# First input projection of a two-layer diffusion backbone: which queue stores the results, and where the second half of the tokens gets its split weights

## The chip, the cores and the metric

One core of a Trainium2 chip runs the whole program. The metric is device time in microseconds (us). The engines are PE (TensorE, matrix products), ACT (ScalarE), DVE (VectorE), POOL (GpSimd) and SP (SyncE, which here only starts DMA transfers). Each engine takes its instructions in order; a DMA transfer is started by the queue of the engine whose name stands in front of `dma_start` (`nc.sync` is SP, `nc.scalar` is ACT).

## The reference

Two layers over 2048 latent tokens and 256 context tokens of 1024 channels. The change lies in the first layer's input projection:

```python
h  = rms_norm(x,  norm_g) * (1 + scale)  + shift
hc = rms_norm(xc, norm_g) * (1 + cscale) + cshift
u  = h @ w_in            # 1024 x 2816; hc the same
a_val, a_gate, q, k, v, z = split(u)      # 512, 512, 512, 128, 128, 1024 columns
q = axial_rope(rms_norm(q, qn_g)); k = axial_rope(rms_norm(k, kn_g))
y_b = attention(q, [ck, k], [cv, v])
y_a = silu(layer_norm(dwconv(a_val * sigmoid(a_gate), 31 taps)))
x = x + gate * (([y_a, y_b] * silu(z)) @ w_out)
```

The second layer (Fourier mixing beside neighbourhood attention) is not touched.

## The kernel before

**Products in three passes.** Every float32 operand of the projection is split into a high part (a rounded copy) and a low part (what is left), both in PE's faster float32 format; a product is high x high + high x low + low x high. For a weight, `load_w` (L383) does this for 256 columns, in two halves of the rows (`kh`): SP loads 512 KB into `wraw` (L390), ACT makes the copy `whi` (L430) and POOL the difference `wlo` (L431). Pool `wp` has four buffers each of `whi` and `wlo`, that is the weights of two tasks; pool `rp` has two of `wraw`, one task.

**Tasks.** `ab_proj` (L434) goes over the 18 tiles of 128 tokens in two halves of three blocks of 384 tokens. In each half eleven tasks (L656) run over the half's blocks, each with 256 columns of the weight: g and u (gate and value of the convolution, twice each), kv (keys and values), q (twice, four heads each) and z (the output gate, four times). The first half's g 0 and u 0 are not in the task loop: they run while the modulation is still being computed, with `w_gu` as their weights. At its start a task takes the weights `ws` that the task before it asked for, and asks for the next task's (`ws_next`). Since every task runs in both halves, each weight is loaded and split twice.

**What a task does with its sums.** g, u and z are six groups of 24 products into one of five PSUM banks (`mm_tile`, L462). ACT evicts a z group with SiLU into `tz` (two buffers), and SP stores it in `gz_d` (L694). In kv and q a group is one tile of 128 tokens; `qk` (L715) takes it through a chain on ACT, DVE and POOL (norm, rotary table `tab` loaded by SP in L719, split), transposes it on PE, and copies it to `sg` on ACT (L759). SP stores v (L752), the queries (L763, four stores a tile) and the keys (L765).

**Convolution.** When both u groups are there, 31 taps per channel group run on DVE (`conv`, L508; L517 is one tap over 1151 or 1168 tokens). They are fed into the stream between the groups of the tasks, some three per group (`advance`, L500; the rates are in L569).

**End of the stage.** At z 0 of the second half `load_kv` (L768) loads keys and values for attention from DRAM into space that the q/k chain has left, again from SP. Attention's first work on DVE is the running maximum L864.

**Order.** The program is written in one order and a planner that simulates the engines fixes each engine's stream ahead of time; within a stream nothing overtakes, on the SP queue neither. Instructions that are ready early may stand well ahead of their place in the text.

Of the kernel before, what the change touches and what calls it, by code (L numbers as in the profile page):

```python
# [20 lines left out]
P = 128  # L21
# [28 lines left out]
def dft_tables():  # L50
    """Cosines and sines of 512 rows for the even and the odd frequencies, and those of a channel group."""
    n, k = np.arange(512, dtype=np.int64), np.arange(1024, dtype=np.int64)
    a = (np.outer(n, k) % 2048) * (2 * np.pi / 2048)
    m = np.arange(128, dtype=np.int64)
    b = (np.outer(m, m) % 128) * (2 * np.pi / 128)
    seq = np.stack([f(a[:, odd::2]) for odd in range(2) for f in (np.cos, np.sin)])
    chan = np.stack([np.cos(b), np.sin(b)])
    return np.ascontiguousarray(seq.astype(np.float32)), chan.astype(np.float32)


class Stream:
    """What is due on each engine in the coming steps."""

# [20 lines left out]
class Build:  # L84
# [56 lines left out]
    def setup(self):  # L141
# [29 lines left out]
        self.gate_d = [self.dram(f"gate{a}", [2, D]) for a in range(2)]  # L171
        self.pat_d = self.dram("pat_d", [9, HEADS, P, 512])

    def x_tile(self, i):
# [3 lines left out]

# [1 line left out]
    def conditions(self, sp, pp, tag):  # L180
# [36 lines left out]
    def adaln(self, layer, j, raw, psum, mo, brow=None):  # L217
        """256 columns of the shift, scale and gate of one layer: in four steps.

        Four column tiles hold sums over a quarter of the rows each, for both conditions.  # L220
        """
        nc, I = self.nc, self.I
# [39 lines left out]

# [1 line left out]
    W0 = [0, 8, 24, 32]  # L264
# [45 lines left out]

# [1 line left out]
    def prep(self, pools, layer, sources, conds, name, eng=None):  # L312
# [70 lines left out]
    def load_w(self, raw_of, wp, w, n0, scale=1.0, eng=None, hold=None, load=True):  # L383
        """High and low parts of 256 columns of a weight, as two halves of its rows."""
        nc = self.nc
        out = []
        for kh in range(2):
            raw = raw_of(kh)
            if load:
                nc.sync.dma_start(  # L390
                    raw, w[kh * 512 : kh * 512 + 512, n0 : n0 + 256].rearrange("(k p) n -> p k n", p=P)
                )
            if scale != 1.0:
                nc.gpsimd.tensor_scalar(out=raw, in0=raw, scalar1=scale, scalar2=1.0, op0=ALU.mult, op1=ALU.mult)
            hi = wp.tile([P, 4, 256], F32R, name="whi", tag="whi")
            lo = wp.tile([P, 4, 256], F32R, name="wlo", tag="wlo")
            if hold is None:
                self.split(hi[:], lo[:], raw, eng or nc.gpsimd)
            else:
                hold.append((hi[:], lo[:], raw, eng or nc.gpsimd))  # L400
            out.append((hi, lo))
        return out

    def raws(self, pool):
        return lambda kh: pool.tile([P, 4, 256], F32, name="wraw", tag="wraw")[:]

    def mm_channel(self, ps, w, h, c, cols, ks=range(KT)):
        """ps[128 channels, tokens] from weight columns c*128.. and a block's columns."""
        nc = self.nc
# [22 lines left out]

# [1 line left out]
    def ab_proj(self):  # L434
# [5 lines left out]
        with ExitStack() as es:  # L440
# [134 lines left out]
            def ada_tiles():  # L575
                """Where the modulation's weights wait, 256 columns at a time: in tiles that nothing else needs yet."""
                quarter = lambda t: t.rearrange("p (k n) -> p k n", n=256)
# [60 lines left out]
            for b in range(3):  # L638
# [8 lines left out]
                for c in range(2):  # L647
                    glu(0, c, b, us[c], sums[1, c, b])
                nxt[b] = hl[b]
            small()  # L650
            ea.close()
# [6 lines left out]
            for half in range(2):  # L658
                blocks = range(3 * half, 3 * half + 3)
                for ti, (kind, j) in enumerate(tasks):  # L660
                    if half == 0 and ti < 2:
                        continue
                    ws = ws_next
                    if half * 11 + ti < 21:
                        nk, nj = tasks[(ti + 1) % 11]
                        ws_next = self.load_w(self.raws(rp), wp, w, col[nk] + 256 * nj)
                    if kind in "guz":
                        for f in late:
# [14 lines left out]
                        for c, b in order:  # L683
# [7 lines left out]
                            else:  # L691
                                t = zp.tile([P, 384], F32, name="tz", tag="tz")
                                nc.scalar.activation(t[:], ps[:, :384], AF.Silu)
                                nc.sync.dma_start(self.gz_d[2 * j + c, :, b * 384 : b * 384 + 384], t[:])  # L694
                            if last and c == 1:
# [19 lines left out]
    def qk(self, qp, q2, q3, sp, pt_p, rope_d, ps, tt, kind, j, nh):  # L715
# [33 lines left out]
        if kind == "kv":  # L749
            vv = q2.tile([P, P], F32, name="vv", tag="vv")  # L750
            nc.scalar.activation(vv[:], ps[:, 128:256], AF.Copy)
            nc.sync.dma_start(self.v_d[tt], vv[:])  # L752
        yield 1
# [7 lines left out]
        if kind == "q":  # L761
            for h in range(4):
                nc.sync.dma_start(self.qs_d[4 * j + h][:, ts], sg[:, h])  # L763
        else:
            nc.sync.dma_start(self.k_d[:, :, ts].rearrange("a p t -> p a t"), sg[:, :2])  # L765

# [1 line left out]
    def load_kv(self):  # L768
        """Keys as [high; high] and as [low; four rows of ones], and values."""
        nc = self.nc  # L770
# [18 lines left out]
    def ab_attention(self):  # L789
        """Scores with the keys on partitions, shifted by each query's greatest score.  # L790

        A unit is two heads of one group for 256 queries. Its greatest scores come from products of one pass, with
        the queries on partitions, a unit ahead; they are rounded and go into the scores as four more rows of the
        contraction, one for each 128 queries.
        """
        nc = self.nc
        with ExitStack() as es:
# [56 lines left out]
            def chunk(i, qt, c):  # L854
                """Part of the least (negated) score of 128 queries."""
                b, hp = units[i]
# [53 lines left out]
            def add(i, k):  # L910
                """Sums over the keys: one on DVE, one on Pool."""
                s = state[i]
# [31 lines left out]
            def total(i):  # L944
                """A row of sums, which DMAs put on 128 partitions for the reciprocals, and copy to all for the products."""
                s = state[i]
# [120 lines left out]

# [1 line left out]
    def load_wout_part(self, raw, w, k, n, eng):  # L1069
        """One block of the rows of half of an output projection's columns."""  # L1070
        ins = self.nc.sync.dma_start(raw, w[k * P : (k + 1) * P, n * 512 : n * 512 + 512])
# [20 lines left out]
    def out_norm(self, psum, b):  # L1092
        """Layer norm and SiLU of the convolution of 256 tokens."""
        nc = self.nc
# [57 lines left out]
    def out_gate(self, b):  # L1152
        """Gates 256 tokens of both branches and splits them."""
        nc = self.nc
# [90 lines left out]

# [1 line left out]
    def cd_proj(self):  # L1247
# [86 lines left out]

# [1 line left out]
    # Rows n and 2048-n, then n and 1024-n, are folded together, so that 512 rows are left for the even and for  # L1336
    # the odd frequencies of the cosine and of the sine part; row 512 is added as a vector of signs.
    def fourier_early(self, psum):
        """What is ready before the last input projections are: channel tables, a table, the first two groups."""
        nc, I = self.nc, self.I  # L1340
# [23 lines left out]
    def fold(self, g, gp, psum):  # L1364
        """A group's folded rows after the channel transform, with rows on partitions."""
        nc = self.nc
# [47 lines left out]
    def dft_table(self, q, rp):  # L1414
        """A quarter of the table of the sequence transform, split."""
        nc = self.nc
# [61 lines left out]

# [1 line left out]
    def natten(self):  # L1480
        nc = self.nc
        with ExitStack() as es:
# [73 lines left out]
            def scores(u):  # L1556
                """The steps of a unit's scores; each gives back its eviction."""
                h, t = u
# [127 lines left out]
            def first_block():  # L1686
                """Gates and splits what is ready of the first block of the output projection."""
                bias.close()
# [45 lines left out]
    def stream(self, q, units, scores, counts, steps, transposes, multiply, lag, off, gap, extra=None):  # L1734
        """Runs the scores of later units beside the products of earlier ones, in a fixed order on each engine."""
        nc = self.nc
# [33 lines left out]

# [1 line left out]
    def cd_out(self):  # L1772
# [101 lines left out]
```

## Time and profile before

| | us |
|---|---|
| runs, fastest, median, slowest of three | 2945.24, 2954.23, 2960.78 |
| profiled execution, span from first to last instruction | 2944.6 |
| of it: start, up to the end of the first products | 0 to 92 |
| of it: tasks of the first projection | 92 to about 740 |
| of it: attention of the first layer and all that follows | from about 740 |

The tables of the profile list an instruction by its line, engine and operation, then output and inputs by the program's names, and a count. In square brackets stands the time that the engine stood idle before it, and what ended that. A line of a helper (L430 and L431, for instance) can serve many places; the names of the tiles tell them apart.

### The profile page before, as it was taken

To read this page: it belongs to the slowest core of one execution; us is meant where nothing else is said; L and a number is where in the kernel's file an instruction comes from. 1 tells how busy PE (TensorE), PEld (TensorE's weight loads), DVE (VectorE), ACT (ScalarE), POOL (GpSimd) and SP (SyncE) were. 2 spreads that over 40 slices of the span, in tenths; PEclk is the share of its full clock that TensorE was granted. 3 is DMA by queue.
4 is the path that set the end of the run, shared out by engine and by line. 5 is a ranking of instruction groups with operands and counts; after the bars stand their busy time and mean duration, and the time that the engine had idled before them with its cause. 6 is when DMAs were issued, how large, how long until landed. Compare 5 with 4: busy or idle time off the path is not lost.

```text
span 2944.6 us, 40977 instructions
## 1 busy us (share of the span) xinstructions
PE 2764.9 (94%) x14481; PEld 2128.3 (72%) x14481; DVE 1855.9 (63%) x2867; ACT 1134.3 (39%) x2103; POOL 1531.5 (52%) x1173
## 2 busy tenths in 40 slices
PE   7988799986999999999999999999999997998998
PEld 5988799886444444444445887988898886888787
DVE  4798869896877788888887564101211336777663
ACT  3223131320354555555554223123222335777421
POOL 3568624846465788778785754222122312455343
PEclk9999899998999999999999999999999998999999
DMA  8224131361642343331123653433333349999852
GB/s 249 91 77 147 53 106 47 96 179 36 196 136 78 123 138 101 90 121 55 51 63 106 235 166 136 150 127 106 126 140 128 111 152 238 220 246 225 273 197 89
DMA packets 345752, 397.66 MB, mean 135 GB/s; under 512 B 54844, under 2 KB 270444, under 8 KB 340555
## 3 DMA queue, kind: packets, MB, share of 16 engines
q1 hardware_dynamic: 344971, 390.85, 44.9%
q10 hardware_dynamic: 576, 4.19, 0.4%
q8 instruction: 114, 1.87, 0.3%
q14 instruction: 91, 0.75, 0.1%
HBM read 270.34 MB, written 129.78 MB: 136 GB/s over the span
## 4 chain that ended last, share of the span: by engine, by line
PE 65%; DMA 11%; DVE 9%; POOL 6%; issue 4%; ACT 1%; SPq 0%; POOLq 0%; ACTq 0%; DVEq 0%
PE av L900 9%; PE s L885 9%; PE mm L415 7%; PE mm L417 7%; PE mm L416 7%; PE m L862 6%; DVE acc L517 5%; DMA nv<-v_d 4%; POOL wlo L431 4%; PE mo L1087 3%; PE mo L1086 3%; PE mo L1085 3%; DMA nk<-k 3%; PE mm L424 2%; PE mm L426 1%
## 5 line engine op out<-in xcount | busy, mean ns | idle before, releaser
L431 POOL TENSOR_TENSOR wlo<-wraw,whi 128x1024 fp32r<-128x1024 f32 x86 | 323.8, 3774 | 499.7 <-ACT whi L430 481.1
L864 DVE TENSOR_REDUCE ast<-m 128x1 f32<-128x512 f32 (+1 forms) x656 | 398.7, 626 | 176.8 <-PE m L862 174.5
L890 ACT ACTIVATE pr<-s 128x512 f32<-128x512 f32 x584 | 343.1, 595 | 298.6 <-PE s L885 253.9
L925 POOL TENSOR_TENSOR accp<-accp,pr 128x512 f32<-128x512 f32 x283 | 398.7, 1409 | 88.1 <-ACT pr L890 74.2
L517 DVE SCALAR_TENSOR_TENSOR acc<-u,cw,acc 128x1151 f32<-128x1151 f32 (+1 forms) x240 | 366.5, 1582 | 0.0
L900 PE MATMUL av<-pr,vt 128*64 128x512 f32 x1168 | 317.4, 622 | 0.0
L417 PE MATMUL mm<-hi_ab,wlo 128*128 128x384 f32 x768 | 260.6, 341 | 39.1 <-POOL wlo L431 39.1
L415 PE MATMUL mm<-hi_ab,whi 128*128 128x384 f32 x768 | 261.0, 346 | 11.6 <-DVE qraw L729 7.2
L416 PE MATMUL mm<-lo_ab,whi 128*128 128x384 f32 x768 | 261.7, 342 | 0.0
L415 PE MATMUL mm<-hi_cd,whi 128*128 128x512 f32 x640 | 250.8, 392 | 1.1 <-ACT hi_cd L379 1.1
L416 PE MATMUL mm<-lo_cd,whi 128*128 128x512 f32 x640 | 250.1, 391 | 0.4 <-DVE lo_cd L380 0.4
L417 PE MATMUL mm<-hi_cd,wlo 128*128 128x512 f32 x640 | 246.7, 390 | 0.0
L417 PEld LDWEIGHTS mm<-hi_ab,wlo 128*128 128x128 f32 x768 | 147.5, 192 | 39.8 <-POOL wlo L431 39.8
L925 DVE TENSOR_TENSOR accd<-accd,pr 128x512 f32<-128x512 f32 x165 | 165.7, 1004 | 0.9 <-ACT pr L890 0.5
L1642 DVE TENSOR_TENSOR nlo<-npt,nhi 128x512 fp32r<-128x512 f32 x192 | 123.6, 644 | 62.1 <-ACT nhi L1640 61.4
L862 PEld LDWEIGHTS m<-k1h,q 128*128 128x128 f32 x328 | 62.2, 190 | 132.9 <-DVE ast L864 84.9
L415 PEld LDWEIGHTS mm<-hi_ab,whi 128*128 128x128 f32 x768 | 147.5, 193 | 14.1 <-DVE qraw L729 7.6
L1604 POOL TENSOR_SCALAR npr<-npr,nst 128x640 f32<-128x640 f32 (+1 forms) x128 | 108.1, 858 | 89.8 <-DVE nst L1603 66.7
L371 DVE TENSOR_SCALAR ht<-ptr,scale,shift 128x384 f32<-128x384 f32 (+2 forms) x96 | 61.2, 671 | 147.4 <-PE ptr L368 146.7
L862 PEld LDWEIGHTS m<-k0h,q 128*128 128x128 f32 x328 | 63.3, 195 | 125.0 <-DVE ast L864 80.6
L430 ACT ACTIVATE whi<-wraw 128x1024 fp32r<-128x1024 f32 x88 | 92.9, 1059 | 148.3 <-PE mm L416 135.5
L416 PEld LDWEIGHTS mm<-lo_ab,whi 128*128 128x128 f32 x768 | 147.8, 193 | 0.8 <-DVE lo_ab L380 0.8
(321 smaller groups left out, 7002.1 us busy)
## 6 DMA issues: line engine op xcount, KB each, us to landing
wraw<-in_cd_w_in_dram SPq DMA_DIRECT2D x46, 512.0 KB, 4.0
wraw<-in_ab_w_in_dram SPq DMA_DIRECT2D x42, 512.0 KB, 3.5
pat_d<-big SPq DMA_DIRECT2D x72, 256.0 KB, 3.7
nk<-k SPq DMA_DIRECT2D x32, 576.0 KB, 12.7
pat<-pat_d SPq DMA_DIRECT2D x24, 768.0 KB, 6.5
nv<-v_d SPq DMA_DIRECT2D x128, 128.0 KB, 7.0
adaraw<-in_ab_w_ada_dram SPq DMA_DIRECT2D x24, 512.0 KB, 6.1
adaraw<-in_cd_w_ada_dram SPq DMA_DIRECT2D x24, 512.0 KB, 3.7
```

Source lines behind the costliest of these rows:

```text
L415: nc.tensor.matmul(ps, a, hh[:, k, cols], start=k == 0, stop=False)
L416: nc.tensor.matmul(ps, a, hl[:, k, cols], start=False, stop=False)
L417: nc.tensor.matmul(ps, b, hh[:, k, cols], start=False, stop=k == KT - 1)
L431: (eng or nc.vector).tensor_tensor(out=lo, in0=src, in1=hi.bitcast(F32), op=ALU.subtract)
L517: ins = nc.vector.scalar_tensor_tensor(out=acc[:, :n], in0=u[:, tap : tap + n], scalar=cw[:, ch, tap : tap + 1], in1=acc[:, :n], op0=ALU.m ...
L862: nc.tensor.matmul(ps[:, :n], lhs, kt[hp // 2][0][:, a : a + n], start=True, stop=True)
L864: nc.vector.tensor_reduce(out=s["st"][:, qt, col : col + 1], in_=ps[:, :n], axis=AX.X, op=ALU.min)
L885: nc.tensor.matmul(ps[:], kt[hp // 2][key][:, k * P : k * P + P], s[x][:].rearrange("p j n -> p (j n)"), start=key == 0, stop=key == 1,)
L890: nc.scalar.activation(pr[:], ps[:], AF.Exp, scale=-1.0)
L900: nc.tensor.matmul(s["av"][x * 64 : x * 64 + 64], vt[:, k - 1 + x, kv * 64 : kv * 64 + 64], s["pr"][k - 1 + x][:], start=k == 1, stop=k == ...
L925: eng.tensor_tensor(out=s[name][:], in0=first_in[:], in1=s["pr"][k][:], op=ALU.add)
L1642: return lambda: nc.vector.tensor_tensor(out=lo[:, :o], in0=pt[:, :o], in1=hi[:, :o].bitcast(F32), op=ALU.subtract)
```

## The change

- The results of the projection, in `gz_d`, `v_d`, `qs_d` and `k_d`, are stored from ACT's queue instead of SP's.
- In the first half each task also stores its split weights in DRAM, four stores of 512 KB (`keep_w`, from SP): high and low part of each half of the rows.
- In the second half, and for the task that leads into it, the next task's weights are read back from there in four loads (`kept_w`, from SP); nothing is loaded raw and nothing is split.

Comment lines and docstrings that went with it are left out here.

```diff
+        self.w_d = [self.dram(f"w_d{i}", [2, 2, P, 1024]) for i in range(11)]
...
+    def keep_w(self, dst, ws):
+
+        for kh, parts in enumerate(ws):
+            for x, t in enumerate(parts):
+                self.nc.sync.dma_start(dst[x, kh], t[:].bitcast(F32).rearrange("p k n -> p (k n)"))
+
+    def kept_w(self, wp, src):
+        out = []
+        for kh in range(2):
+            parts = [wp.tile([P, 4, 256], F32R, name=n, tag=n) for n in ("whi", "wlo")]
+            for x, t in enumerate(parts):
+                self.nc.sync.dma_start(t[:].bitcast(F32).rearrange("p k n -> p (k n)"), src[x, kh])
+            out.append(tuple(parts))
+        return out
...
+            for i in range(2):
+                self.keep_w(self.w_d[i], w_gu[i])
             small()
...
                     ws = ws_next
-                    if half * 11 + ti < 21:
-                        nk, nj = tasks[(ti + 1) % 11]
+                    if half == 0:
+                        self.keep_w(self.w_d[ti], ws)
+                    nk, nj = tasks[(ti + 1) % 11]
+                    if half * 11 + ti < 10:
                         ws_next = self.load_w(self.raws(rp), wp, w, col[nk] + 256 * nj)
+                    elif half * 11 + ti < 21:
+                        ws_next = self.kept_w(wp, self.w_d[(ti + 1) % 11])
...
-                                nc.sync.dma_start(self.gz_d[2 * j + c, :, b * 384 : b * 384 + 384], t[:])
+                                nc.scalar.dma_start(self.gz_d[2 * j + c, :, b * 384 : b * 384 + 384], t[:])
...
-            nc.sync.dma_start(self.v_d[tt], vv[:])
+            nc.scalar.dma_start(self.v_d[tt], vv[:])
...
-                nc.sync.dma_start(self.qs_d[4 * j + h][:, ts], sg[:, h])
+                nc.scalar.dma_start(self.qs_d[4 * j + h][:, ts], sg[:, h])
...
-            nc.sync.dma_start(self.k_d[:, :, ts].rearrange("a p t -> p a t"), sg[:, :2])
+            nc.scalar.dma_start(self.k_d[:, :, ts].rearrange("a p t -> p a t"), sg[:, :2])
```

## The prediction

> **What bounds the kernel now.** I read the page first, then the busy time of each engine by stage, then the list of waits inside the stage that the change touches, and last the timeline around the two longest waits of TensorE.
>
> ```profile
> span 2944.6 us, 40977 instructions
> PE 2764.9 (94%) x14481; PEld 2128.3 (72%) x14481; DVE 1855.9 (63%) x2867; ACT 1134.3 (39%) x2103; POOL 1531.5 (52%) x1173
> ```
>
> PE is busy 94% of the span, but a mean over stages hides where the rest is. The same by stage (first projection's start, its main part, everything behind it); columns after the stretch and its length are busy PE, PEld, DVE, ACT, POOL with instruction counts, then granted clock, DMA share and GB/s:
>
> ```profile
> 0.00:92.00 92.00, 71.14 (x465) 59.10 (x466) 43.59 (x102) 31.99 (x60) 34.55 (x68) 0.98 0.74 222
> 92.00:740.00 648.00, 568.57 (x3635) 560.33 (x3633) 531.99 (x618) 157.52 (x331) 378.51 (x224) 0.94 0.31 93
> 740.00:2944.00 2204.00, 2125.19 (x10384) 1508.84 (x10384) 1280.34 (x2148) 944.80 (x1712) 1118.43 (x881) 0.98 0.49 144
> ```
>
> The projection runs to about 740 us. From 92 to 740 PE is idle for 648 - 568.6 = 79.4 us: all that an edit of this stage can win by filling gaps. Behind it PE is idle 79 us in 2204, so what the projection saves should reach the end. What holds PE up is in the list of waits of that stretch (us in total, times, longest) and, in order of time, at its two longest gaps:
>
> ```profile
> PE mm L417 <- POOL wlo L431: 39.1, 2, 23.7
> ACT tz L693 <- DMA gz_d<-tz: 71.4, 7, 38.7
> ```
>
> ```profile
> 355.58 0.69 PE L417 MATMUL mm<-hi_ab,wlo 128*128 128x384 f32 x1 [15.38 <-POOL wlo L431]
> 708.30 0.69 PE L417 MATMUL mm<-hi_ab,wlo 128*128 128x384 f32 x1 [23.74 <-POOL wlo L431]
> ```
>
> Two waits make 39.1 of the 79.4 us, one in each half of the tokens, both at the start of the last gate task (z 3). The instruction that ends them, first as a group (shortest, median and longest in ns), then the two themselves, and VectorE beside the second:
>
> ```profile
> L431 POOL TENSOR_TENSOR wlo<-wraw,whi x86: 2349/2402/47767, 97.6 to 2358.5; 128x1024 fp32r<-128x1024 f32 x86
> 313.82 41.71 POOL L431 TENSOR_TENSOR wlo<-wraw,whi 128x1024 fp32r<-128x1024 f32 x1 [18.83 <-ACT whi L430]
> 660.48 47.77 POOL L431 TENSOR_TENSOR wlo<-wraw,whi 128x1024 fp32r<-128x1024 f32 x1 [24.31 <-ACT whi L430]
> 627.64 78.41 DVE L517 SCALAR_TENSOR_TENSOR acc<-u,cw,acc 128x1168 f32<-128x1168 f32 x55
> 735.22 0.76 DVE L864 TENSOR_REDUCE ast<-m 128x1 f32<-128x256 f32 x2 [29.17 <-PE m L862]
> ```
>
> The low part of z 3's weights is a subtraction on GpSimd, 2.40 us by its median; these two took 41.71 and 47.77 us. Both lie in an unbroken run of convolution taps on VectorE: 55 taps in 78.41 us from 627.64, and GpSimd's instruction ends at 708.25, 2.2 us after the last tap. GpSimd gets nowhere while VectorE has no gap.
>
> **What the change removes.** The second half splits no weights: its 22 subtractions on GpSimd and 22 copies on ScalarE go. First term: the 23.74 us wait at 708.30. The 15.38 us of the first half stay, since that half still splits.
>
> ```profile
> 425.00:498.00 73.00, 73.00 (x429) 73.00 (x428) 54.77 (x42) 11.13 (x15) 23.48 (x6) 1.00 0.14 44
> 498.00:602.00 104.00, 90.26 (x707) 88.41 (x706) 93.38 (x147) 31.64 (x83) 79.83 (x76) 0.93 0.33 96
> 660.00:706.00 46.00, 24.57 (x142) 24.25 (x140) 46.00 (x35) 4.68 (x9) 45.52 (x1) 0.81 0.10 35
> 706.00:738.00 32.00, 27.50 (x146) 27.10 (x146) 2.75 (x7) 2.94 (x6) 4.57 (x2) 0.90 0.15 51
> ```
>
> Second: after that wait the granted clock is 0.90 and a matmul costs 27.50/146 = 0.188 us, against 73.00/429 = 0.170 at full clock; 146 x 0.018 = 2.6 us.
>
> Third, the query and key tasks of the second half (498 to 602): PE is idle 104 - 90.26 = 13.7 us, VectorE and GpSimd are both near full, and six subtractions lie among them.
>
> ```profile
> 597.54 2.35 POOL L431 TENSOR_TENSOR wlo<-wraw,whi 128x1024 fp32r<-128x1024 f32 x1 [0.42 <-ACT whi L430]
> 597.85 2.31 DVE L741 TENSOR_TENSOR t<-t,qsq 128x256 f32<-128x256 f32 x1
> 614.50 0.41 DVE L741 TENSOR_TENSOR t<-t,qsq 128x256 f32<-128x256 f32 x1
> 627.64 12.46 DVE L517 SCALAR_TENSOR_TENSOR acc<-u,cw,acc 128x1168 f32<-128x1168 f32 x6
> ```
>
> Beside a subtraction the sum L741 took 2.31 us, otherwise 0.41: 1.9 us lost. Six times that is 11.4 us of VectorE, and PE can get back 13.7 at most, nothing at least. I take 5, under half, because only a delay that stands in the chain of a token tile reaches PE, and five PSUM banks hide the rest.
>
> Fourth, the gate stores. In SP's queue they stand behind loads that wait:
>
> ```profile
> 637.32 10.16 SPq L694 DMA_DIRECT2D gz_d<-tz  x2
> 637.32 15.27 DMA gz_d<-tz
> 653.23 0.45 PE L415 MATMUL mm<-hi_ab,whi 128*128 128x384 f32 x1 [1.89 <-ACT tz L693]
> 627.41 1.16 SPq L779 DMA_DIRECT2D k0h<-k_d  x2
> ```
>
> ScalarE waits 71.4 us for such stores, yet PE loses only 1.89 at 653.23, as in the first half the subtraction is the later of the two. Term: 1.9 us. The Trainium skill, "DMA: Bandwidth & Descriptors", section "Issuing engines are not separate DMA queues", speaks against this part: transfers started by ScalarE and SyncE run on the same 16 engines, and a second starter saves only issuing time. By it the 1.9 us would stay and the sum be 25.3 instead of 27.2; the 10.16 us that two issues took on SP suggest that issuing is what was stuck.
>
> **What it adds.** In the first half 44 stores of 512 KB (23 MB); in the second 44 loads of 512 KB in place of 22.
>
> ```profile
> wraw<-in_ab_w_in_dram SPq DMA_DIRECT2D x42, 512.0 KB, 3.5
> out_dram<-qo SPq DMA_DIRECT2D x16, 512.0 KB, 2.8
> SPq L390 <- POOL wlo L431: 336.8, 70, 38.9
> ```
>
> A task's four stores take 4 x 2.8 = 11 us of transfer at most, beside 24 us of matmuls, where DMA is a third busy. SP then waits for the low part before it goes on; it does so today already (336.8 us in L390's waits), so the new wait mostly stands where the old one stood. Behind it wait the next raw weights, the tables of the q/k norms, input blocks and convolution stores. Price for the first half: from 0 to the 12.5 us of the first rival; I take 2, near nothing, as the stored tiles are split a task earlier in all but z 3.
>
> In the second half a set can be loaded only when PE has left the buffers of two tasks back: 4 x 3.5 = 14 us at most, in 25 us. One place is tight: z 2's set stands on SP behind the key and value loads. These are six of 0.59 MB (64 rows of 2304 floats) and one of 1.18, 4.7 MB together; the gate store behind them landed at 637.32 + 15.27 = 652.59, so they took 25.2 us from 627.41, 187 GB/s. At that rate z 2's 2.1 MB take 11.2 us more, to 663.8, with the first half of the rows by 658.2. PE needs them from about 655, and has 2 us of work on the first rows. Price 0 to 9 us; I take 4.
>
> ScalarE's new issues, where they are many:
>
> ```profile
> 587.95 1.74 SPq L763 DMA_DIRECT2D qs<-sg  x4
> 590.73 0.42 ACT L744 ACTIVATE hl<-t 128x256 fp32r<-128x256 f32 x1 [2.80 <-DVE t L741]
> 591.05 0.37 ACT L722 ACTIVATE qsq<-mm 128x256 f32<-128x256 f32 x1
> 591.31 0.59 ACT L759 ACTIVATE sg<-ptr 128x512 f32<-128x512 f32 x1
> L1477 ACTq DMA_DIRECT2D yc<-yf x4: 326/326/344, 2409.1 to 2443.0; - x4
> ```
>
> A query tile stores four times: 1.74 us on SP, 4 x 0.326 = 1.3 by the only row on ScalarE's queue. After sg ScalarE is idle 2.80 us until the next tile's sum comes, so I cost the issues at nothing; without that cover they cost 1.74 us a tile.
>
> Sum: -23.7 - 2.6 - 5 - 1.9 + 2 + 4 = **-27.2 us**. Late next would be VectorE: today its last tap ends 29.17 us ahead of attention's first maximum, so the end of the projection cannot move by more than 29.2 plus what VectorE itself gains (12.46 - 6 x 1.346 = 4.4 us in the row of six taps, and up to 11.4 above).
>
> **Rivals.** (1) The starvation moves into the first half.
>
> ```profile
> 99.97 0.38 SPq L390 DMA_DIRECT2D wraw<-in_ab_w_in_dram  x1
> 105.69 5.27 POOL L431 TENSOR_TENSOR wlo<-wraw,whi 128x1024 fp32r<-128x1024 f32 x2
> 113.53 23.99 DVE L517 SCALAR_TENSOR_TENSOR acc<-u,cw,acc 128x1151 f32<-128x1151 f32 x18
> ```
>
> The weights of u 1 are loaded from 99.97 and subtracted from 105.69 to 111, just ahead of 18 dense taps (113.53 to 137.5). Stores put ahead of that load on SP would push the subtraction past the run's start, and PE, which wants these weights near 125, would wait 12.5 us. With the full 9 us at z 2 and nothing from the third term: -28.2 + 12.5 + 9 = -7, 2947 us. For it: the few microseconds of margin. Against it: the stored tiles are ready early. The Trainium skill, "SBUF — State Buffer", section "Who interferes with whom", says that the port pair of VectorE and GpSimd is locked for one whole instruction; by that rule GpSimd would get in behind the tap in flight, after 1.4 us, and this rival would cost next to nothing. The 41.71 us do not bear that out here. Chance 0.20.
>
> (2) Slower: ScalarE's query stores lie in the chain. 36 query tiles (nine in each of two tasks, in both halves) x 1.74 = 62.6 us, less 27.2: +35, 2990 us. It decides from 27.2/36 = 0.76 us a tile. The row of 2.80 us idle speaks against it; for it, that ScalarE's queue is in order and these issues stand ahead of hl and qsq. Chance 0.07.
>
> (3) The kept weights come late in every task of the second half, and the wait for GpSimd becomes one for DMA: 2.5 us in each of 11 tasks eats the gain, 2954 us. Against it: 14 of 25 us. Chance 0.08.
>
> (4) More: all 13.7 us of the query tasks and nothing lost, -42, 2912 us. Chance 0.10.
>
> **How the numbers follow.** The sum is made on a span of 2944.6 us, 0.6 below the fastest of the three runs (2945.24); I put it on their median, 2954.2 - 27.2 = **2927 us**, chance 0.55. A measurement of this kernel tells about 0.5% (14.8 us) from no change. Range 2911 to 2948: below it only more than rival 4, above it rivals 2 and 3. Faster: 0.55 + 0.10 + a third of rival 1 = 0.71; same: the rest of 1, and 3, 0.22; slower: 0.07.
>
> **What would show it.** Right: no wait for GpSimd at z 3 of the second half, the first half's 15 us still there, no subtraction after about 360 us until the second layer, attention's first maximum near 708 instead of 735, ScalarE free of waits for gate stores. Wrong: PE waits for kept weights at z 2 of more than 9 us, for u 1's low part near 125, ScalarE no longer idle before hl in the query tasks, or VectorE's taps still running when PE has finished.

## The result and the profile after

| us | before | changed |
|---|---|---|
| median of four runs each | 2957.39 | 2909.96 |
| fastest, slowest | 2945.24, 2960.78 | 2907.36, 2916.09 |
| profiled span | 2944.6 | 2905.6 |

The ratio is 0.9845, 95% interval 0.9821 to 0.9869: the changed kernel is faster, by 47 us in the medians and 39.0 in the spans.

The head of the changed kernel's page:

```profile
span 2905.6 us, 40946 instructions
PE 2752.1 (95%) x14481; PEld 2118.0 (73%) x14481; DVE 1825.2 (63%) x2867; ACT 1116.8 (38%) x2081; POOL 1416.4 (49%) x1151
```

PE ran the same 14481 products. GpSimd has 22 instructions less and is 115 us less busy, far more than 22 x 2.4 us: long, starved subtractions have gone. Where the time went is read from where the projection's products lie, by tile (line, engine, operation, tiles; shortest, median and longest in ns; first and last start). First the two forms before, then after:

```profile
L417 PE MATMUL mm<-hi_ab,wlo x768: 331/334/688, 29.4 to 734.7; 128*128 128x384 f32 x192
L425 PE MATMUL mm<-wlo,hi_ab x432: 277/283/522, 152.8 to 597.4; 128*128 128x256 f32 x144
```

```profile
L433 PE MATMUL mm<-hi_ab,wlo x768: 331/334/689, 28.8 to 684.4; 128*128 128x384 f32 x192
L441 PE MATMUL mm<-wlo,hi_ab x432: 277/283/542, 152.2 to 578.8; 128*128 128x256 f32 x144
```

The first form serves g, u and z, the second keys and queries. By these last starts the key and query products of the second half are done 18.6 us earlier (578.8 for 597.4), the last z product 50.3 us earlier (684.4 for 734.7). Behind it the span gives 11 us back.

By stage, in order of the products (us; "start" runs to the first key product of the second half, kv' to q1' are that half's key and query tasks, z' its four gate tasks, each from its first start to its last end; the last column is what lies behind):

| kernel | start | kv' to q1' | z 0' z 1' z 2' z 3' | end | behind |
|---|---|---|---|---|---|
| before | 496.0 | 104.6 | 30.0 28.9 25.1 51.0 | 735.1 | 2209.5 |
| changed | 490.6 | 89.7 | 27.6 25.1 27.0 25.1 | 684.7 | 2220.9 |

The waits of PE by the engine that ended them (total, count, longest), before, over the key and query tasks of the second half:

```profile
PE ptr L757 <- ACT hl L747: 4.2, 1, 4.2
PE mm L424 <- DVE qraw L729: 3.6, 3, 2.0
PE ptr L757 <- DVE hl L745: 3.2, 2, 2.5
PE mm L415 <- DVE qraw L729: 2.5, 1, 2.5
```

The same tasks after:

```profile
PE mm L440 <- DVE qraw L751: 2.9, 4, 0.8
PE mm L431 <- DVE qraw L751: 0.8, 1, 0.8
PE ptr L779 <- DVE hl L767: 0.3, 1, 0.3
```

From 13.5 us of waits 4.0 are left. The stage's windows, before and then after (columns as in the prediction), show that this isn't all:

```profile
496.00:600.60 104.60, 90.86 (x716) 89.01 (x714) 94.03 (x146) 31.93 (x83) 80.43 (x75) 0.93 0.32 94
```

```profile
491.00:580.70 89.70, 85.64 (x715) 84.22 (x714) 74.72 (x143) 26.93 (x77) 61.98 (x68) 1.00 0.43 135
```

PE's idle time falls from 13.7 to 4.1 us (9.7), and its busy time, for the same products, from 90.9 to 85.6 (5.2), because the granted clock is 1.00 and no longer 0.93 (the last section shows where it was lost).

In the gate tasks of the second half, after, PE's longest waits, and then rows of the timeline (start, length; idle time before in brackets), of which the first two lie in the first half:

```profile
PE mm L433 <- DMA wlo<-w_d: 1.3, 2, 0.7
```

```profile
310.70 44.20 POOL L447 TENSOR_TENSOR wlo<-wraw,whi 128x1024 fp32r<-128x1024 f32 x2 [14.70 <-ACT whi L446]
352.61 0.69 PE L433 MATMUL mm<-hi_ab,wlo 128*128 128x384 f32 x1 [15.53 <-POOL wlo L447]
607.37 8.72 ACTq L785 DMA_DIRECT2D qs<-sg  x4
605.76 75.47 DVE L533 SCALAR_TENSOR_TENSOR acc<-u,cw,acc 128x1168 f32<-128x1168 f32 x56
684.87 1.09 DVE L886 TENSOR_REDUCE ast<-m 128x1 f32<-128x256 f32 x3 [3.64 <-PE m L884]
```

The wait of 23.74 us is gone, that of the first half stands (15.53), and the taps end at 681.2, 3.64 us ahead of attention's first maximum where it was 29.17. One row is new: ScalarE's queue took 8.72 us from the first to the last of the four stores of one query tile. The four issues themselves make 1.6 us of it; for the other 7.1 us the queue shows nothing. PE lost nothing by it here; the run with ScalarE stores only shows what it can cost.

### The profile page after: what moved, and what is told of

Its sections match the earlier page's. It is cut to its first block, busy times and chain, and to the rows that moved or that the text cites. A ratio compares the mean times of both kernels' runs of the same rounds, so it can differ in the third digit from the quotient of the medians.

```text
span 2905.6 us, 40946 instructions
## 1 busy us (share of the span) xinstructions
PE 2752.1 (95%) x14481; PEld 2118.0 (73%) x14481; DVE 1825.2 (63%) x2867; ACT 1116.8 (38%) x2081; POOL 1416.4 (49%) x1151
## 4 chain that ended last, share of the span: by engine, by line
PE 62%; DMA 10%; DVE 3%; POOL 2%; issue 2%; ACT 1%; SPq 0%; POOLq 0%; ACTq 0%; DVEq 0%
PE av L922 9%; PE s L907 8%; PE mm L431 6%; PE mm L433 6%; PE mm L432 6%; PE m L884 6%; PE mo L1107 4%; PE mo L1108 4%; PE mo L1109 4%; DMA nv<-v_d 3%; DMA nk<-k 3%; PE mm L442 1%; PE mm L441 1%; PE mm L440 1%; DMA pat<-pat_d 1%
## 5 line engine op out<-in xcount | busy, mean ns | idle before, releaser
L447 POOL TENSOR_TENSOR wlo<-wraw,whi 128x1024 fp32r<-128x1024 f32 x64 | 202.4, 3169 | 380.3 <-ACT whi L446 380.2
L533 DVE SCALAR_TENSOR_TENSOR acc<-u,cw,acc 128x1151 f32<-128x1151 f32 (+1 forms) x240 | 353.0, 1526 | 0.0
L433 PEld LDWEIGHTS mm<-hi_ab,wlo 128*128 128x128 f32 x768 | 145.5, 190 | 17.8 <-POOL wlo L447 15.8
L431 PEld LDWEIGHTS mm<-hi_cd,whi 128*128 128x128 f32 x640 | 120.4, 188 | 26.1 <-ACT hi_cd L380 1.6
```

Source lines behind the costliest of these rows:

```text
L431: nc.tensor.matmul(ps, a, hh[:, k, cols], start=k == 0, stop=False)
L433: nc.tensor.matmul(ps, b, hh[:, k, cols], start=False, stop=k == KT - 1)
L447: (eng or nc.vector).tensor_tensor(out=lo, in0=src, in1=hi.bitcast(F32), op=ALU.subtract)
L533: ins = nc.vector.scalar_tensor_tensor(out=acc[:, :n], in0=u[:, tap : tap + n], scalar=cw[:, ch, tap : tap + 1], in1=acc[:, :n], op0=ALU.m ...
```

## The experiments

The theory: the gain is GpSimd's subtractions alone, as one of them is starved (shut out while they run) by VectorE's taps and six others slow the key and query chain. The rivals: that the stores on ScalarE's queue carry a part, that ScalarE's copies or the raw loads do, or that the price is a matter of when a subtraction starts. All kernels compute the whole reference. Times in us, medians; "before" is the old kernel on the same chip. Rows with "one run" have no interval; of them only "before again" has more than one run of the old kernel beside it.

| run | this | before | ratio (95%) | start | kv' to q1' | z' | end | behind |
|---|---|---|---|---|---|---|---|---|
| before again | 2951.67 | 2959.22 | one run | 495.1 | 104.7 | 134.5 | 734.3 | 2215.5 |
| changed again | 2912.78 | 2955.78 | 0.9854 (0.9838 to 0.9871) | 489.1 | 89.7 | 102.9 | 681.7 | 2222.4 |
| kept weights only | 2910.87 | 2959.22 | 0.9841 (0.9819 to 0.9863) | 495.3 | 86.8 | 105.5 | 687.6 | 2222.1 |
| ScalarE stores only | 2982.78 | 2959.22 | 1.0078 (1.0055 to 1.0101) | 495.4 | 102.5 | 154.7 | 752.6 | 2233.3 |
| before, z 3 on VectorE | 2924.74 | 2959.22 | 0.9886 (0.9862 to 0.9909) | 485.8 | 105.1 | 108.7 | 699.6 | 2227.6 |
| query weights kept | 2960.73 | 2966.15 | one run | 496.2 | 92.1 | 135.6 | 723.9 | 2235.1 |
| gate weights kept | 2930.11 | 2966.15 | one run | 495.4 | 102.3 | 102.4 | 700.1 | 2228.2 |
| low part kept | 2905.81 | 2966.15 | one run | 490.7 | 87.8 | 102.6 | 681.1 | 2222.9 |
| high part kept | 2977.27 | 2966.15 | one run | 492.7 | 105.9 | 155.3 | 753.9 | 2221.6 |
| changed, z 3 on VectorE | 2898.29 | 2955.78 | 0.9804 (0.9789 to 0.9819) | 479.1 | 89.6 | 104.6 | 673.3 | 2224.1 |
| changed, q and z 3 on VectorE | 2895.90 | 2955.78 | 0.9799 (0.9783 to 0.9814) | 473.6 | 89.7 | 103.1 | 666.4 | 2229.1 |
| low part kept, z 3 on VectorE | 2902.51 | 2955.78 | 0.9825 (0.9803 to 0.9847) | 486.8 | 88.9 | 102.4 | 678.1 | 2222.4 |

### Both kernels again

> The kernel before, profiled once more. Up to the end of the first projection the two profiles of the changed and the old kernel differ by 50 us, at the end of the span by 39: 11 us are given back in the last tenth of the program, which the change does not touch. Theory 1 (chance): the first profile of the old kernel, 2944.6 us, was a lucky one there; this one takes 5 to 15 us longer in that part and has the same first projection within 2 us. Theory 2 (the change costs something late): this profile agrees with the first one within 3 us everywhere.

> The changed kernel once more, as the base of the next three: 2905 to 2917 us.

The stages repeat within 1 us in kv' to q1' and 1.5 in z'. Behind the projection the old kernel took 2209.5 and 2215.5 us, the changed one 2220.9 and 2222.4, and the other kernels 2221.6 to 2235.1, for the same code. So the 11 us given back in the first pair are in good part chance: the profiled run of the old kernel was the fastest of its four, 12 us under their median, and by the medians the change brings 47 of the 50 us that it gains at the projection's end. Whether the change costs some 5 us there stays open: both of its values lie above both old ones, as do those of the other ten kernels, but two old profiles are few.

### The two parts apart

Kept weights with all stores from SP:

```diff
-    nc.scalar.dma_start(self.gz_d[...], t[:])
+    nc.sync.dma_start(self.gz_d[...], t[:])
...
-                nc.scalar.dma_start(self.qs_d[4 * j + h][:, ts], sg[:, h])
+                nc.sync.dma_start(self.qs_d[4 * j + h][:, ts], sg[:, h])
```

(v and k the same.)

> Weights kept as in the change, all results stored from SP as before. Theory A (the splits themselves): nearly the whole gain is here, 40 to 46 us of the 47, and the query tasks of the second half are as short as in the changed kernel (from the end of u 1 to the end of q 1 some 13 to 15 us shorter than before). Theory B (the queue): the second half's query tasks are no shorter than before, the gain is that of z 3 alone, 26 to 30 us.

Measured: 0.9841, the same as the whole change; the key and query tasks are 17.8 us shorter than before, more than the 13 to 15 expected. The gate stores do wait on SP again, and here is what PE pays for it: among ACT's waits from 90 to 790 us, and PE's in the gate tasks,

```profile
ACT tz L715 <- DMA gz_d<-tz: 85.9, 10, 36.8
```

```profile
PE mm L431 <- ACT tz L715: 1.5, 1, 1.5
```

85.9 us of ScalarE cost PE 1.5. On ScalarE's queue that 1.5 is gone, but the key and query tasks take 89.7 instead of 86.8.

The stores alone, nothing kept:

```diff
-                self.keep_w(self.w_d[i], w_gu[i])
...
-                    if half == 0:
-                        self.keep_w(self.w_d[ti], ws)
...
-                    if half * 11 + ti < 10:
+                    if half * 11 + ti < 21:
                         ws_next = self.load_w(self.raws(rp), wp, w, col[nk] + 256 * nj)
```

> Results stored from ScalarE, weights loaded raw and split in both halves as before. Theory A: 0 to 7 us faster, both long subtractions still there (over 35 us each), query tasks shorter by less than 3 us in each half. Theory B: 15 to 20 us faster, with query tasks of both halves shorter by 6 us or more. The rival that ScalarE's issues lie in the chain: slower, by up to 60 us.

Measured: slower than before, by 23 us, so neither theory A nor B holds for this kernel; only the rival of ScalarE's issues had the sign. What the gate stores alone bring is there: from the first product of z 0' to that of z 2' it takes 52.3 us where before took 58.5. But z 2' takes 77.5 us and z 3' 25.1, where before had 25.1 and 51.0. The timeline of this kernel around it:

```profile
624.69 74.12 DVE L533 SCALAR_TENSOR_TENSOR acc<-u,cw,acc 128x1168 f32<-128x1168 f32 x55
625.58 8.92 ACTq L781 DMA_DIRECT2D qs<-sg  x4
634.55 0.50 ACT L711 ACTIVATE tz<-mm 128x384 f32<-128x384 f32 x1 [9.00 <-DMA qs<-sg]
634.93 1.06 ACT L446 ACTIVATE whi<-wraw 128x1024 fp32r<-128x1024 f32 x1
636.07 67.28 POOL L447 TENSOR_TENSOR wlo<-wraw,whi 128x1024 fp32r<-128x1024 f32 x2 [19.22 <-ACT whi L446]
```

and the same two steps in the kernel before:

```profile
628.35 1.05 ACT L430 ACTIVATE whi<-wraw 128x1024 fp32r<-128x1024 f32 x1
629.47 6.70 POOL L431 TENSOR_TENSOR wlo<-wraw,whi 128x1024 fp32r<-128x1024 f32 x2 [10.06 <-ACT whi L430]
```

ScalarE can't go on until its four stores are issued, 8.92 us. The issues themselves make 1.8 us of that; between the second and the third the queue shows nothing for 6.9 us, and SP's queue, which is starting the large key and value loads, stands still at the same time (625.1 to 631.1). So the copy for z 2 comes 6.6 us later, and the two subtractions behind it, 6.70 us in the kernel before, take 67.28. Both pairs start inside the run of taps (627.64 and 624.69); the brackets differ, 10.06 us of idle GpSimd ahead of the one and 19.22 ahead of the other, and the last section comes back to them. PE waited for them 50.4 us, the longest of its waits for POOL's `wlo`. That the stores cause the delay is shown by the run, that they do it through this step is read from the trace. The kept weights remove what hangs on that step, so the two parts of the change don't add up: +23 alone, about nothing beside the kept weights.

### One subtraction on VectorE

The kernel before, with only z 3's low part subtracted on VectorE, in both halves:

```diff
-    ws_next = self.load_w(self.raws(rp), wp, w, col[nk] + 256 * nj)
+    ws_next = self.load_w(self.raws(rp), wp, w, col[nk] + 256 * nj, eng=nc.vector if (ti + 1) % 11 == 10 else None)
```

> The kernel before with one edit: the low part of z 3's weights is subtracted on VectorE instead of GpSimd, in both halves; nothing is kept, stores from SP. If GpSimd is shut out by the dense taps and nothing else is wrong at z 3: both waits of PE go (15.4 and 23.7 us) against about 5 us of VectorE work in its own queue, 30 to 42 us faster, without any weight in DRAM. If the two subtractions are long for another reason (their inputs come late, or z 3 has to wait for VectorE's queue anyway): under 15 us faster.

Measured: 34 us faster, without a byte kept. The same subtraction on the engine that starved it:

```profile
650.88 1.22 DVE L447 TENSOR_TENSOR wlo<-wraw,whi 128x1024 fp32r<-128x1024 f32 x1 [4.20 <-ACT whi L446]
655.85 45.85 DVE L533 SCALAR_TENSOR_TENSOR acc<-u,cw,acc 128x1168 f32<-128x1168 f32 x34
701.61 1.08 DVE L882 TENSOR_REDUCE ast<-m 128x1 f32<-128x256 f32 x3
```

1.22 us in place of 47.77. But in this kernel VectorE ends the stage: its taps run to 701.7 and the maximum follows at once, while PE is done at 699.6. The key and query tasks stay at 105.1, which marks the rest of the change's gain.

### Which tasks

Weights kept for q 0, q 1 and z 0 alone (`ti in (5, 6, 7)`), then for z 1 to z 3 alone (`ti in (8, 9, 10)`); all others are split again:

```diff
-                    if half == 0:
+                    if half == 0 and ti in (5, 6, 7):
                         self.keep_w(self.w_d[ti], ws)
```

> The changed kernel with only the three sets kept whose splits fall into the second half's key and query tasks (q 0, q 1, z 0); all others are split in both halves. From the first product of kv to the first of z 0 in the second half the old kernel takes 104.6 us, the changed one 89.7, the one with ScalarE stores and no kept weights 102.5. If the splits inside this stage are what lengthens it: 92 or less here. If it is what lies before or behind: 100 or more. z 1 to z 3 split on GpSimd again, so one wait of PE for it comes back, 20 to 50 us.

> The changed kernel with only z 1, z 2 and z 3 kept. No wait of PE for GpSimd in the second half; the key and query stage of the second half 100 us or more if the splits in it lengthen it, 92 or less if it is anything else. Time 25 to 35 us under the old kernel by the first, 45 by the second.

Measured: the first shortens kv' to q1' by 12.5 us (104.6 to 92.1, a tenth above the bound set for it) and keeps a wait of 30.6 us at z 3'. The second leaves kv' to q1' at 102.3 and has all four gate tasks at 25.1 to 27.5. So each effect goes with its own sets of weights. In the spans the projection's end moves by 11 and 35 us. That this makes 46 of the change's 50 is in part chance: z 0' and z 1' are 6 us shorter in both runs, and z 3' is 7 us longer in the first than before, as PE reaches it 18 us earlier but the taps end only 11 us earlier.

### Which instruction

In the second half the raw weights are loaded and only one part comes from DRAM. Low part kept, the high one copied on ScalarE as before:

```diff
+            self.nc.sync.dma_start(raw, w[...])
...
-            for x, t in enumerate(parts):
-                self.nc.sync.dma_start(..., src[x, kh])
+            self.nc.scalar.activation(parts[0][:], raw, AF.Copy)
+            self.nc.sync.dma_start(..., src[1, kh])
```

> The changed kernel, but in the second half only the low parts come from DRAM; the raw weights are loaded and copied to the high part on ScalarE as before, GpSimd subtracts nothing there. If GpSimd's subtraction (and VectorE waiting beside it) lengthens the key and query stage: 93 us or less, as in the changed kernel. If ScalarE's copy, which waits for PE with the tiles' work behind it, does: 100 us or more. No wait of PE for GpSimd at z 3 in either case.

High part kept, the low one subtracted on GpSimd as before:

```diff
+            self.nc.sync.dma_start(..., src[0, kh])
+            self.nc.gpsimd.tensor_tensor(out=parts[1][:], in0=raw, in1=parts[0][:].bitcast(F32), op=ALU.subtract)
```

> The mirror of it: in the second half the high parts come from DRAM, the low parts are subtracted on GpSimd from the raw weights; ScalarE copies nothing there. If GpSimd's subtraction lengthens the key and query stage: 100 us or more; if ScalarE's copy does: 93 or less. A wait of PE for GpSimd of 20 us or more at z 2 or z 3 in either case, so slower than the changed kernel by 20 to 60 us.

Measured: 2905.81 and 2977.27, one run each. With ScalarE's copies and the raw loads back, nothing of the gain is lost; with the subtraction back, all of it is. The windows of the key and query tasks, low part kept and then high part kept:

```profile
490.80:578.60 87.80, 85.17 (x716) 84.22 (x715) 73.75 (x140) 30.71 (x79) 60.55 (x68) 1.00 0.47 140
```

```profile
492.60:598.50 105.90, 91.85 (x716) 90.08 (x714) 90.08 (x148) 26.48 (x76) 75.24 (x73) 0.92 0.39 117
```

With the subtractions back, both the gaps and the clock of 0.92 are back. And in the gate tasks of the second kernel a subtraction is starved again. It came late because it waited for PE to leave its buffer:

```profile
626.31 74.91 DVE L535 SCALAR_TENSOR_TENSOR acc<-u,cw,acc 128x1168 f32<-128x1168 f32 x54
652.46 52.30 POOL L418 TENSOR_TENSOR wlo<-wraw,whi 128x1024 fp32r<-128x1024 f32 x1 [21.11 <-PE mm L435]
```

Begun 26 us into 74.91 us of taps, it ends 3.5 us behind the last of them; PE waited 50.7 us, at z 2. With the ScalarE stores' 50.4 this is the second kernel in which z 2 pays and z 3 doesn't, for another reason of being late. The price is what is left of the run of taps, not the size of the work.

### Versions that go further

The changed kernel with the first half's z 3 on VectorE, then with q 0, q 1, z 0 and z 3, then with z 3 on VectorE and only low parts stored and read:

```diff
-    ws_next = self.load_w(self.raws(rp), wp, w, col[nk] + 256 * nj)
+    ws_next = self.load_w(self.raws(rp), wp, w, col[nk] + 256 * nj, eng=nc.vector if (ti + 1) % 11 in (5, 6, 7, 10) else None)
```

> The changed kernel with the first half's z 3 split on VectorE. If the first half's wait at z 3 is the same starvation: PE's 15.5 us go; some 4 to 6 us come back in the next stage (the first tasks of the second half grew by 5.8 us when the old kernel was edited in this way), so 8 to 13 us under the changed kernel. If the taps left over make VectorE late at the end of the projection: under 5 us.

> As that, and q 0, q 1 and z 0 of the first half are also split on VectorE (1.22 us a piece instead of 2.4 on GpSimd). If GpSimd's subtractions lengthen the key and query stage as in the second half (105.7 us now against 89.7): 95 us or less there and 15 to 25 us under the changed kernel in all. If VectorE's own time is what counts: the stage as long as now, total as the run with z 3 alone.

> Only the low parts are kept and read back, the high parts are copied on ScalarE in both halves, and the first half's z 3 is split on VectorE. If DMA traffic of the high parts costs anything: 1 to 5 us under the run with z 3 on VectorE and everything kept. If not: equal to it within 3 us.

Measured: 2898.29, 2895.90 and 2902.51, beside 2912.78 for the changed kernel in the same batch. The first two are faster than both kernels and not told apart from each other; the runs of the third (2899.50 to 2913.69) overlap those of the changed one (2905.82 to 2914.29). z 3 of the first half falls from 45.6 to 28.0 us, but the task behind it (g 0 of the second half) takes 38.5 instead of 33.5, so some 12 of 17.6 us remain; the time falls by 14.5 us where 8 to 13 were expected. The query weights on VectorE bring little: the first half's key and query tasks take 101.3 us instead of 105.7, short of the 95 expected if GpSimd alone held them. Their windows, changed kernel and then this one:

```profile
152.50:258.20 105.70, 92.27 (x715) 90.49 (x715) 94.62 (x154) 31.80 (x83) 77.39 (x74) 0.92 0.47 149
```

```profile
153.60:254.90 101.30, 89.24 (x717) 87.41 (x715) 89.74 (x157) 31.44 (x82) 63.26 (x68) 0.97 0.49 155
```

GpSimd is 14 us less busy, yet PE still idles 12.1 us where it idled 13.4. VectorE, busy 89.74 of 101.3 us, ends 7.6 us of PE's waits in this stage and ScalarE 4.4, so VectorE is the likelier hold in this half; that wasn't tried further. Storing only low parts saves 22 of the 44 added stores (the second half still has 44 loads) and is no faster than storing both: 2902.51 is 4.2 us above 2898.29, more than the 3 us allowed for "equal", and its first half's key and query tasks take 111.5 us. That the high parts' stores cost anything isn't shown.

## Why the prediction was right, and where its size was off

The direction and the named place were right: faster, z 3's wait in the second half gone, the first half's left. The size was not that of the likeliest case: 47 us by the medians where 27.2 were forecast, and 2909.96 lies 1 us below the range. What came is close to rival 4 (all of the query tasks' idle time and nothing lost, 2912, chance 0.10), and 5 us of clock beside it. By its steps, in the profiled pair:

- **z 3' (-23.7 and -2.6).** z 3' fell from 51.0 to 25.1, 25.9 us for 26.3. Right, and shown by the runs that keep only z weights and only low parts.
- **Key and query tasks (-5, nothing to 13.7).** This is the term that was mis-sized: 14.9 us, above the upper end. The step that failed is "I take 5, under half, because only a delay that stands in the chain of a token tile reaches PE": 9.7 of 13.7 us of idle time went. And the upper end itself was too low, as it held only the idle time. The row from which it came had a clock of 0.93 in it; the clock was priced behind z 3 and not here, where it is worth 5.2 us (9.7 + 5.2 = 14.9). That the subtractions are the cause is shown from both sides: low part kept 87.8, high part kept 105.9.
- **Gate stores (-1.9).** The wait was read rightly, its price was not: z 1' fell by 3.8 us, twice the wait, as its clock was 0.94 before and is 1.00 after. The run with the stores alone has z 1' at 25.0 too. Beside kept weights, stores from SP leave a wait of 1.5 us in z 1'; stores from ScalarE leave none, but the key and query tasks take 2.9 us more. The Trainium skill, "DMA: Bandwidth & Descriptors", section "Issuing engines are not separate DMA queues", says that a second starter saves only issuing time; in total the runs agree that nothing more is to be had (ratio 0.9841 without, 0.9845 with), though the wait that was to stay by it went. ScalarE itself isn't free of waits for gate stores, as the prediction had it: 27.4 us are left of 71.4, at no cost to PE.
- **ScalarE's issues (nothing).** The row on which that rested (0.326 us an issue) doesn't hold for the queue as a whole: 8.72 us for four at one place. Nor is the 2.80 us of cover named there what made it free. In the run with low parts kept, four stores take 8.43 us on that queue and ScalarE still copies the high parts behind them, and z 2' takes 25.0 us: what is missing there is a subtraction on GpSimd behind the copy. Rival 2 put its price on the 36 tiles; the run with the stores alone shows one tile in one place, worth 50 us.
- **Stores of the first half (+2).** Too high: up to the second half's key tasks the changed kernel is 5.4 and 6.9 us ahead of before, not behind; with SP's stores it is 0.7 ahead, and before itself moved by 0.9 between two profiles. What gave the 5 us wasn't separated.
- **Kept z 2 behind the key loads (+4, 0 to 9).** 1.9 us in one profile, 0.2 in the other. The bound was safe, the value high.
- **Late next.** VectorE, as named, now ends only 3.5 us ahead of PE. The bound was too tight: attention's first maximum comes 50.3 us earlier (684.87 for 735.22), where 29.2 + 4.4 + 11.4 = 45.0 was the most allowed, as the last tap ends 24.8 us earlier where 15.8 was the most allowed.
- **z 0'**, which the sum didn't have, gave 2.4 us: a wait of 2.23 us for VectorE is gone. It is gone with the stores alone too (27.3), so it isn't the kept weights' doing by itself.
- **Rival 1** didn't come. In the changed kernel u 1's second subtraction did slip into the taps, as that rival has it, but took 3.49 us and PE did not wait for it:

```profile
112.64 1.65 POOL L339 TENSOR_TENSOR st<-st,mhalf 128x1 f32<-128x1 f32 x1
114.39 1.82 POOL L340 TENSOR_SCALAR xt<-xt,st 128x1024 f32<-128x1024 f32 x1
116.17 3.49 POOL L447 TENSOR_TENSOR wlo<-wraw,whi 128x1024 fp32r<-128x1024 f32 x1
```

  So the prediction's sentence "GpSimd gets nowhere while VectorE has no gap" is too broad: at this place GpSimd did get in behind the tap in flight, as the prediction drew from the Trainium skill, "SBUF — State Buffer", section "Who interferes with whom". The last section says where it didn't.

Taken together: -25.9 - 14.9 - 5.4 - 2.4 - 3.8 + 1.9 = -50.5, for -50.4 at the projection's end; then +11.4 behind it in this pair of spans, which makes -39.0.

## What to carry to other kernels

In the timeline of GpSimd, look for an instruction far above its median inside a run of taps on VectorE, with a long idle time in its bracket, before weighing a larger change: moving z 3's subtractions (one argument) brought 34 us where the whole change brought 47. The two aren't the same time: some 10 of the 34 come from the first half, whose wait at z 3 the change leaves. Time each part of a change by itself: here one part cost 23 us alone and about nothing beside the other. Where PE has many short gaps, price the granted clock of that stage as well as its idle time.

## What was not expected of the hardware

- **Starvation goes with GpSimd's idle time.** The run that kept only query weights has both outcomes in one run of 55 taps, VectorE's row first:

```profile
616.23 78.41 DVE L533 SCALAR_TENSOR_TENSOR acc<-u,cw,acc 128x1168 f32<-128x1168 f32 x55
```

```profile
628.22 3.28 POOL L447 TENSOR_TENSOR wlo<-wraw,whi 128x1024 fp32r<-128x1024 f32 x1 [8.29 <-ACT whi L446]
646.16 50.68 POOL L447 TENSOR_TENSOR wlo<-wraw,whi 128x1024 fp32r<-128x1024 f32 x1 [14.67 <-ACT whi L446]
```

  The first found GpSimd idle for 8.29 us and got in behind the tap in flight; the second, after 14.67 us, stayed out and ended at 696.84, 2.2 us behind the last tap. It is so throughout. In the 14 profiles 90 subtractions began during a tap with at least four more taps to come at once. The 61 that began within 10.43 us of GpSimd's work before took at most 3.62 us; the 29 that began 13.40 us or more behind it took 7.89 to 64.94, to the end of the run. How far into the run they began doesn't part them: ten taps in, one took 12.94 us (idle 15.87, before) and one 3.52 (idle 6.61, changed). The Trainium skill, "SBUF — State Buffer", section "Who interferes with whom", says that the port pair which VectorE and GpSimd share is an exclusive lock, and that "Whoever issues first gets the shared pair for the whole instruction". If it comes free behind each tap, the 61 agree with that and the 29 don't. VectorE pays nothing for the 29: 74.12 / 55 = 1.348 us a tap beside the longest, 75.47 / 56 = 1.348 in the changed kernel without one. No run changed the idle time alone, so whether a small instruction that keeps GpSimd awake would do what the kept weights do wasn't tried, and the cause stays open.
- **Short gaps went with half the clock.** With 13.7 us of PE's 104.6 idle, in waits of at most 4.2 us, the granted clock was 0.93; with 4.1 us idle, in waits of 0.8 at most, it was 1.00. The kernel before, in stretches within the key and query tasks, and the last line in z 1':

```profile
511.00:517.80 6.80, 5.03 (x24) 5.03 (x24) 6.30 (x15) 2.26 (x9) 4.03 (x8) 0.50 0.30 80
517.80:524.00 6.20, 6.20 (x54) 6.20 (x53) 4.38 (x11) 2.23 (x8) 4.11 (x7) 1.00 0.27 76
654.40:657.70 3.30, 3.30 (x12) 3.30 (x12) 3.30 (x4) 0.96 (x2) 0.00 (x0) 0.50 0.25 91
```

  The clock is not a little lower all along; it is halved for 6.8 us from 511.0, within the wait of 4.2, for 6.8 more from 572.4, between waits of 2.5 and 2.0, and for 3.4 behind the wait of 1.89 in z 1'. The six profiles of kernels that subtract on GpSimd in the second half's key and query tasks have 13.7 us or more at half clock there, the other eight none. The length of one wait doesn't decide it: those of 2.5 and 2.2 us in z 0' left the clock at 1.00.
- **Issuing can take microseconds.** Four stores of 64 KB took ScalarE's queue 8.72 and 8.92 us beside SP's large loads; the issues themselves made 1.6 and 1.8 us of that, in the rest the queue stood still.
- **The same code behind the projection took 2209.5 to 2235.1 us** over 14 profiles, so one profile's span can't settle a change of less than 1% here.
